# A norm factor that is left out of an MLP's operands and put into the norm behind it, on one Trainium2 core

## The chip, the cores and the metric

The kernel runs on one core of a Trainium2 chip. The core has a matrix engine (PE, TensorE), a vector engine (DVE), an activation engine (ACT, ScalarE), a general engine (POOL, GpSimd), and SyncE (SP), which issues most of the transfers (DMA) between device memory and the on-chip memory (SBUF). Each engine takes its instructions in the order of the program; semaphores hold an instruction back until its operands are there and the place it writes is free. The metric is the time of one execution on the device in microseconds (us).

## What is computed

Two layers of a streaming encoder for 1024 + 32 tokens of width 1024: a forgetting attention (FoX), then a gated linear recurrence (HGRN2), each followed by an MLP with a squared ReLU and hidden width 4096. Cut to what the change touches, for each layer:

```python
def rmsnorm(x, g):
    return x * lax.rsqrt(jnp.mean(x * x, axis=-1, keepdims=True) + EPS) * g

x = x + rmsnorm(out, post_mix_norm[layer])     # out: the mixer's output projection
h = rmsnorm(x, pre_ffn_norm[layer])            # x * r * gain, r one number per token
u = jax.nn.relu(h @ ffn_w_up[layer])
x = x + rmsnorm((u * u) @ ffn_w_down[layer], post_ffn_norm[layer])
```

With r left out of h, relu(x * gain @ W) is smaller by r and its square by r squared, and the norm behind the MLP can make up for that: the mean of squares is multiplied by the fourth power of r ahead of the root, and its factor by r squared.

## The kernel before

Tokens lie along the free axis, features on the partitions. The 1056 tokens are four blocks of G = 264; half c (0 or 1) of the tokens is two of them (h = 0, 1), so that an operation on one feature tile of one half is 128 x 528. Everything that the change touches is in `tail`, which runs once behind each mixer: output projection, norm of the mixer, input norm of the MLP, MLP, norm behind it.

*The MLP.* The products go by a scheme of seven products on 2 x 2 blocks (Strassen's), each product in three passes on split operands (high times high, high times low, low times high). A half's input has four pairs of feature tiles (kp = 0 to 3). `forms` makes, for each pair, the scaled tiles (a DVE operation with the gain of the feature and the factor r of the token), four differences (`t_forms`) and the split into high (a cast on ACT) and low (DVE): the tile F[c][kp], 2 x 7 x 264 wide. `unit` runs the seven products, `unit8` (for half 0's first NA = 5 units, and half 1's last steps) the same matrix in eight plain products, m by m. `block` issues the matmuls, `cut` splits weights into S. The 16 units of the up projection go: units 0 to 4 on half 0 alone (`up8`), then unit i on both halves with unit i - 5 on half 1. Results, squared, go as forms to device memory (`uf`), and `get_forms` fetches them in four parts for each pair and half (forms 0-1, 2-3, 4-5, 6) through four landing places in the tile st. The four slots of F for each half are used again, pair p in slot p % 4. `down` has 19 steps: 0 to 13 on both halves, 14 to 18 on half 0, then `down8` 14 to 18 on half 1.

*The factor.* `sums` (called cs in the profile) adds the squares over the partitions with a matmul against ones; `factor` takes the root: two ACT operations and three on DVE for each block, and with `sc` (a factor of the mixer's own, in layer 1) three DVE operations more. `postnorm` goes over the eight feature tiles: scale (DVE), add to x (DVE), square the new x (ACT), add the square to a sum (DVE).

*The order around the change.* The output projection of half 0 goes first, then column 0 of half 1's, then half 0's factor and `postnorm` on DVE while PE goes on with columns 1 to 4. Then cs for the second factor stands on PE between columns 4 and 5, `forms` of half 0 comes on DVE and ACT, PE goes on with columns 5 to 7 and begins unit 0. Half 1's factor stands in unit 0, its second between units 1 and 2; its forms must be there at unit 5. At the end of the MLP half 0's norm runs while half 1's last steps are on PE; `next_h` makes the next mixer's input. A scheduler lays the instructions out; `soon` gives priority, `behind` and `pin` fix an order by hand.

## Time and profile before

| | |
|---|---|
| median of 3 runs | 3012.45 us (3007.43 to 3015.72) |
| the profiled execution | 3009.45 us, its span 3007.7 us |
| busy: PE, DVE | 2845.7 us (95%), 2053.5 us (68%) |
| busy: ACT, POOL | 1472.0 us (49%), 1468.6 us (49%) |
| waits of PE for F casts (L316), for squares ahead of cs, for the first result of half 1 in `down` | 15.5, 34.4, 15.2 us |
| transfers | 349.36 MB, 116 GB/s on the mean |

The profile page gives each engine's busy time and the span in 40 slices; the trace behind it answers for any stretch. Three views carry what follows. A table by windows has the busy time and the number of instructions of each engine in a stretch, the granted clock of PE as a share of its full 2.4 GHz, and the transfers. A timeline has one engine's instructions in order, each with the idle time before it and what ended that. A view of one source line has the durations of its operations by shape.

### The profile page before, as it was taken

What the parts mean: (1) busy time and instruction counts of PE and PEld (TensorE: products, weight loads), DVE (VectorE), ACT (ScalarE), POOL (GpSimd) and SP (SyncE); (2) the same over time, 40 slices, a digit from 0 to 9 for tenths busy, and PEclk for the clock granted to TensorE, in tenths of its full rate; (3) what the DMA queues carried; (4) which work ended last, traced back from release to release, by engine and by line L of the source; (5) the groups of instructions that cost most, each with busy time, mean ns of one, the idle gap of its engine ahead of it and who ended that gap; (6) DMA issues with size and microseconds to landing.
All of it is one profiled execution on the core that took longest, in us unless ns stands there. A gap on an engine that the chain in (4) does not pass through costs nothing.

```text
span 3007.7 us, 56032 instructions
## 1 busy us (share of the span) xinstructions
PE 2845.7 (95%) x21377; PEld 2725.1 (91%) x21377; DVE 2053.5 (68%) x3419; ACT 1472.0 (49%) x3104; POOL 1468.6 (49%) x1595
## 2 busy tenths in 40 slices
PE   7999999999889998999979999999988999899987
PEld 6888888899889998999869999999988999799986
DVE  6788888864785545678888655546488554667787
ACT  6455555555455655544454232322345665644443
POOL 2344444431227775466723644544314886556660
PEclk9999999999989999999989999999999999899997
DMA  5111211144434445445353211115444443544452
GB/s 163 47 48 46 55 46 48 52 113 142 137 129 173 158 145 183 153 132 152 111 161 118 57 56 40 48 33 150 145 126 161 154 166 144 192 143 135 148 166 76
DMA packets 329172, 349.36 MB, mean 116 GB/s; under 512 B 19535, under 2 KB 287703, under 8 KB 328903
## 3 DMA queue, kind: packets, MB, share of 16 engines
q1 hardware_dynamic: 327879, 345.65, 36.6%
q8 instruction: 168, 2.75, 0.4%
q14 instruction: 101, 0.83, 0.1%
q0 software_dynamic: 1024, 0.13, 0.0%
HBM read 238.78 MB, written 106.88 MB: 115 GB/s over the span
## 4 chain that ended last, share of the span: by engine, by line
PE 70%; DVE 13%; DMA 5%; ACT 4%; issue 4%; POOL 4%; SPq 0%; DVEq 0%; ACTq 0%; POOLq 0%
PE mA L410 14%; PE mB L410 11%; PE hj L184 8%; PE pj L184 8%; PE mE L410 5%; PE gp L184 4%; PE po L184 4%; DMA st<-uf 2%; DVE S L398 2%; PE mD L410 1%; DVE F L317 1%; PE lv L1465 1%; POOL hs L310 1%; PE pv L1129 1%; PE ss L1002 1%
## 5 line engine op out<-in xcount | busy, mean ns | idle before, releaser
L410 PE MATMUL mA<-F,S 128*128 128x264 f32 x4404 | 604.8, 289 | 50.3 <-ACT F L316 15.5
L410 PEld LDWEIGHTS mA<-F,S 128*128 128x128 f32 x4404 | 566.0, 191 | 62.8 <-ACT F L316 17.2
L410 PE MATMUL mB<-F,S 128*128 128x264 f32 x4248 | 585.5, 287 | 11.1 <-DVE S L398 4.8
L410 PEld LDWEIGHTS mB<-F,S 128*128 128x128 f32 x4248 | 548.4, 191 | 17.5 <-DVE S L398 9.0
L398 DVE TENSOR_TENSOR S<-Sx,S 128x512 fp32r<-128x512 f32 (+3 forms) x280 | 247.6, 889 | 157.3 <-ACT S L397 155.0
L398 DVE TENSOR_TENSOR S<-raw,S 128x512 fp32r<-128x512 f32 (+3 forms) x282 | 240.4, 857 | 89.6 <-ACT S L397 89.5
L317 DVE TENSOR_TENSOR F<-st,F 128x528 fp32r<-128x528 f32 (+2 forms) x260 | 229.1, 885 | 100.0 <-ACT F L316 99.3
L316 ACT CAST F<-st 128x528 fp32r<-128x528 f32 (+2 forms) x260 | 153.6, 596 | 252.4 <-DMA st<-uf 238.6
L410 PE MATMUL mE<-F,S 128*128 128x264 f32 x1740 | 246.4, 289 | 17.9 <-DVE S L398 9.3
L184 PE MATMUL pj<-H,wh 128*128 128x352 f32 x1152 | 256.7, 341 | 2.1 <-POOL wh L163 1.5
L336 POOL TENSOR_TENSOR Sx<-raw 128x512 f32<-128x512 f32 (+3 forms) x140 | 187.9, 1345 | 132.1 <-DVE S L398 129.6
L410 PEld LDWEIGHTS mE<-F,S 128*128 128x128 f32 x1740 | 225.3, 190 | 26.2 <-DVE S L398 14.5
L310 POOL TENSOR_TENSOR hs<-hs 128x264 f32<-128x264 f32 x216 | 188.4, 891 | 103.5 <-ACT hs L549 101.0
L184 PE MATMUL hj<-h,wh 128*128 128x264 f32 x1600 | 228.7, 289 | 0.0
L170 POOL TENSOR_SCALAR wh<-wr 128x1024 fp32r<-128x1024 f32 x58 | 69.0, 1190 | 319.2 <-PE hj L184 100.2
L184 PEld LDWEIGHTS pj<-H,wh 128*128 128x128 f32 x1152 | 199.8, 192 | 19.0 <-POOL wh L163 1.7
L200 POOL TENSOR_TENSOR e<-e,Y 128x264 f32<-128x264 f32 x170 | 164.0, 974 | 102.1 <-ACT e L741 87.3
L171 DVE TENSOR_TENSOR wl<-wr,wh 128x1024 fp32r<-128x1024 f32 x102 | 135.3, 1328 | 111.1 <-POOL wh L170 59.4
L184 PEld LDWEIGHTS hj<-h,wh 128*128 128x128 f32 x1600 | 206.1, 189 | 1.6
L397 ACT CAST S<-Sx 128x512 fp32r<-128x512 f32 (+3 forms) x280 | 163.6, 585 | 51.3 <-PE mE L410 22.1
L397 ACT CAST S<-raw 128x512 fp32r<-128x512 f32 (+3 forms) x282 | 161.3, 574 | 45.4 <-PE mB L410 32.5
L1125 DVE TENSOR_TENSOR pl<-pf,ph 128x512 fp32r<-128x512 f32 x192 | 127.6, 669 | 54.2 <-POOL ph L1124 29.7
(351 smaller groups left out, 5879.0 us busy)
## 6 DMA issues: line engine op xcount, KB each, us to landing
st<-uf SPq DMA_DIRECT2D x192, 264.0 KB
uf<-hs SPq DMA_DIRECT2D x54, 924.0 KB
raw<-in_ffn_w_up_dram SPq DMA_DIRECT2D x40, 1024.0 KB
raw<-in_ffn_w_down_dram SPq DMA_DIRECT2D x30, 1024.0 KB
wr<-in_hgrn_w_in_dram SPq DMA_DIRECT2D x39, 512.0 KB
wr<-in_fox_w_in_dram SPq DMA_DIRECT2D x32, 512.0 KB
uf<-us SPq DMA_DIRECT2D x10, 924.0 KB
st<-uf SPq DMA_DIRECT2D x64, 132.0 KB
```

The lines of the kernel that those rows point to most:

```text
L170: self.g.tensor_scalar(out=wh, in0=raw, scalar1=1.0, scalar2=0.0, op0=ALU.mult, op1=ALU.add)
L171: self.v.tensor_tensor(wl, raw, wh.bitcast(F32), op=ALU.subtract)
L184: ins = self.nc.tensor.matmul(ps, lhsT=ws[kk][a], rhs=xs[kk][b], start=i == 0, stop=i == tot - 1)
L200: self.g.tensor_tensor(out, a, b, op=op)
L310: ins = e.tensor_tensor(f[:, o], f[:, a], f[:, b], op=ALU.subtract)
L316: self.s.copy(hi, src)
L317: self.v.tensor_tensor(lo, src, hi.bitcast(F32), op=ALU.subtract)
L336: self.g.tensor_tensor(src, a, b, op=op)
L397: self.s.copy(hi, src)
L398: self.v.tensor_tensor(lo, src, hi.bitcast(F32), op=ALU.subtract)
L410: ins = self.nc.tensor.matmul(o, lhsT=a[:, i], rhs=F[kp % 4][:, b, f], start=start and n == 0, stop=stop and n == tot - 1, skip_group_chec ...
L1125: self.v.tensor_tensor(pl[:, :N], pf[:, :N], ph[:, :N].bitcast(F32), op=ALU.subtract)
```

## The change

1. `forms` no longer takes r. It runs for one pair; the scaling by the gain alone is an ACT copy with a scale. For half 0, pairs 0 and 1 are made inside `postnorm` (through the new argument `then`), pairs 2 and 3 directly behind it. All of half 1's projection columns run without a cs in between.
2. `square_factor` makes r, squares it with one DVE operation and keeps it in the tile rq. For half 0 its cs comes behind the projection, for half 1 behind unit 4. `factor` behind the MLP takes it as `sc`.
3. At the first step of `down` the parts are fetched in another order: the parts of forms 0 and 1 of pairs 0 and 1 and of both halves first.
4. Half 1's pairs 14 and 15 are fetched in three parts each (forms 0, 1, 2 and 4, all that `down8` reads), and pair 15's go to places of pairs 13 and 14 that are no longer read (`moved`, `operand`), ahead of the half-0 steps.
5. `next_h(0)` goes into the middle of `down8(16)` (through `mid`).
6. The weights of the last step go to the upper rows of the buffer that the step before uses. The tile rr has one buffer where it had three.

```diff
@@ -281,6 +282,9 @@
                     todo[j - 1] = self.square(c, x[:, j - 1, sl], j - 1, hs, tmp)
             if j >= 2 and more:
                 put(todo[j - 2](self.v))
+            if then and 1 < j <= NJ and j % 2 == 0:
+                for ins in then(j // 2 - 1):
+                    put(ins)
 
     def xd_view(self):
         return self.xd.rearrange("p j (h c t) -> p j h c t", h=2, c=2)
...
-                                                  op0=ALU.mult, op1=ALU.mult)
-                if last:
-                    self.behind(ins, last)
-            last = self.t_forms(f, (self.v, self.v, self.v, self.v))
-            self.F[c].append(place(kp))
-            self.split(self.F[c][kp], f[:, 0:7], 0, 7)
+
+    def forms(self, c, x, kind, layer, kp, f, F):
+        for j, o in ((2 * kp, f[:, 0:8:7]), (2 * kp + 1, f[:, 2:5:2])):
+            self.s.activation(o, x[:, j], AF.Copy, scale=self.gcol(kind, layer, j))
+        ins = self.t_forms(f, (self.v, self.v, self.v, self.v))
+        self.F[c].append(F)
+        return ins, self.split(F, f[:, 0:7], slice(0, 7))
 
 
 
...
@@ -387,6 +386,9 @@
                 if e == 1:
                     with self.soon():
                         evac(m, e, 1, z)
+                    if m == 0 and self.mid:
+                        f, self.mid = self.mid, None
+                        f(self.last_mm)
 
     def bank(self, tag):
...
 
 
+    def operand(self, F, kp, b, f):
+        if F is self.F[1] and (kp, f) in self.moved:
+            kp, f = self.moved[kp, f]
+        return F[kp % 4][:, b, f]
+
...
         for a, b in ((hi, 1), (lo, 1), (hi, 0)):
             for i, kp in enumerate(pairs):
-                ins = self.nc.tensor.matmul(o, lhsT=a[:, i], rhs=F[kp % 4][:, b, f], start=start and n == 0,
...
 
+            r2 = [tp.tile([128, 2, G], F32, name=f"rq{layer}_{c}") for c in range(2)]
+
+            def square_factor(c, late):
+                r = self.factor(self.acc(c), late=late, r=r2[c])
+                self.v.tensor_tensor(r, r, r, op=ALU.mult)
+
...
             with ExitStack() as c2:
                 ob = self.pool(f"ob{layer}", 1, ctx=c2, side="right")
-                ya = new(fa, "ya", 28)
-                ys = [pair(ya)]
-                xa = pair(new(fa, "xa", 16))
-
-                scr = [ob.tile([128, 8, G], F32, name=f"fs{layer}_{i}") for i in range(2)]
+                ys = [pair(new(fa, "ya", 16))]
+                scr = new(fa, "fs", 8)
+                new(fa, "pad", 4)
+                xa = new(ob, "xa", 16)
+                xw, xa = xa[:, 0:8], pair(xa)
 
                 def project(c, os, hs=(0, 1)):
                     for o in os:
...
                 self.get_x(0, xa)
-                scs = sc and sc(0)
+                scs = sc and sc(0, r2[0])
                 project(0, range(NJ))
                 ys.append(pair(new(self.rh if last else ob, "yb", 16)))
                 late = project(1, range(1))
                 fr = self.factor(self.acc(0), scs, late=late)
                 self.pin(self.last_cs)
-                self.postnorm(0, ys[0], xa, fr, 1, layer)
+
+                put = lambda kp: self.forms(0, xa, 2, layer, kp, scr if kp < 3 else xw, form_tile(fa))
+                self.postnorm(0, ys[0], xa, fr, 1, layer, then=lambda kp: put(kp) if kp < 2 else ())
                 self.put_x(0, xa)
-                late = project(1, range(1, 5))
-                r = self.factor(self.acc(0), late=late)
-                self.pin(self.last_cs)
-                self.forms(0, xa, r, 2, layer, lambda kp: scr[kp % 2], lambda kp: form_tile(fa))
-                project(1, range(5, NJ))
+                put(2)
+                put(3)
+                square_factor(0, project(1, range(1, NJ)))
 
 
                 xb = pair(new(self.rh, "xb", 16))
...
                 up8(0, ust, lambda m: first[m])
-                fr = self.factor(self.acc(1), sc and sc(1), late=self.mid_mm)
+                fr = self.factor(self.acc(1), sc and sc(1, r2[1]), late=self.mid_mm)
                 self.pin(self.last_cs)
...
-                if i == 1:
-                    r = self.factor(self.acc(1), late=self.last_mm)
-                if i == 2:
-                    self.pin(self.last_cs)
             with self.soon():
-                self.forms(1, xb, r, 2, layer, lambda kp: (fscr, st)[kp % 2], lambda kp: form_tile(fb, tag=f"f{kp}"))
+                for kp in range(4):
+                    self.forms(1, xb, 2, layer, kp, fscr, form_tile(fb, tag=f"f{kp}"))
+            square_factor(1, self.last_mm)
             n = [0]
 
```

```diff
 
-            def get_forms(p, c, n=4):
-                for a, b in ((0, 2), (2, 4), (4, 6), (6, 7)):
+            PARTS = ((0, 2), (2, 4), (4, 6), (6, 7))
+
+            def get_forms(p, c, parts=PARTS):
+                for a, b in parts:
                     self.nl += 1
-                    i = 8 - 2 * (self.nl % n + 1)
+                    i = 8 - 2 * (self.nl % 4 + 1)
                     t = st[:, i:i + b - a]
                     nc.sync.dma_start(t, self.uf[p][c][:, a:b])
-                    self.split(self.F[c][p % 4], t, a, b)
+                    F, o = self.F[c][p % 4], slice(a, b)
+                    if c and (p, a) in self.moved:
+                        q, o = self.moved[p, a]
+                        F, o = self.F[c][q % 4], slice(o, o + 1) if b == a + 1 else slice(o, o + 3, 2)
+                    self.split(F, t, o)
 
...
             for s in range(LAG):
-                for p in range(4) if s == 0 else (s,) if s > 3 else ():
+                if s == 0:
+
+                    for p, part in zip((0, 1, 0, 1, 2, 0, 0, 1, 1, 2, 2, 2, 3, 3, 3, 3),
+                                       (0, 0, 1, 1, 0, 2, 3, 2, 3, 1, 2, 3, 0, 1, 2, 3)):
+                        for c in range(2):
+                            get_forms(p, c, parts=(PARTS[part],))
+                elif s > 3:
                     for c in range(2):
-                        get_forms(p, c)
+                        get_forms(s, c)
                 down(s, (0, 1), load)
-            get_forms(LAG, 1)
+            few = ((0, 2), (2, 3), (4, 5))
+            get_forms(LAG, 1, parts=few)
+
+            self.moved = {(15, 0): (14, 3), (15, 1): (14, 5), (15, 2): (14, 6), (15, 4): (13, 6)}
+            get_forms(15, 1, parts=few)
             for s in range(LAG, 19):
                 if s < 16:
                     get_forms(s, 0)
-                down(s, (0,), load)
-
-
+                down(s, (0,), load if s < 18 else lambda src: load(src, 4))
+
+
+            new(fa, "pad", 28)
             xs = [pair(new(fa, "xs", 16)) for c in range(2)]
             for c in range(2):
...
+            fr = self.factor(self.acc(0), r2[0], late=self.mid_mm)
             self.postnorm(0, Y[0], xs[0], fr, 3, layer, more=not last)
             down8(15, 1, load2)
             if last:
                 self.store_y(0, xs[0], yring)
             else:
-                next_h(0, self.last_mm)
+                self.mid = lambda late: next_h(0, late)
             for s in range(16, 19):
-                down8(s, 1, load2)
+                down8(s, 1, load2 if s < 18 else lambda src: load2(src, 4))
             if last:
                 fr = None
                 for h in range(2):
-                    fr = self.factor(self.acc(1), r=fr, hs=(h,))
+                    fr = self.factor(self.acc(1), r2[1], r=fr, hs=(h,))
                     self.postnorm(1, Y[1], xs[1], fr, 3, layer, more=False, hs=(h,))
                     self.store_y(1, xs[1], yring, (h,))
                 return
@@ -815,7 +846,7 @@
             self.cut(w0[1], w0[0], raw)
             c4.close()
             late = self.hgrn_early(w0, ev)
-            fr = self.factor(self.acc(1), late=late[0])
+            fr = self.factor(self.acc(1), r2[1], late=late[0])
```

On PE in layer 0 the middle of half 1's projection stood like this before (po: a column's result, H and wh, wl: operands of the projection, cs: the sum of squares):

```order
L184 MATMUL po_9692<-H_78,wl_9663 128x264 x8
L184 MATMUL po_9692<-H_79,wh_9662 128x264 x8
L219 MATMUL cs_9721<-st_8881,ones 128x264
L219 MATMUL cs_9729<-st_8881,ones 128x264
L184 MATMUL po_9779<-H_78,wh_9775 128x264 x8
L184 MATMUL po_9779<-H_78,wl_9776 128x264 x8
```

and the start of the MLP behind the projection (F_918 to F_921: half 0's pairs 0 to 3, mA, mB, mE: products of unit 0):

```order
L184 MATMUL po_9925<-H_78,wl_9896 128x264 x8
L184 MATMUL po_9925<-H_79,wh_9895 128x264 x8
L410 MATMUL mA_9966<-F_918_9743,S_9964 128x264
L410 MATMUL mA_9966<-F_919_9752,S_9964 128x264
L410 MATMUL mB_9967<-F_918_9743,S_9964 128x264
L410 MATMUL mB_9967<-F_919_9752,S_9964 128x264
L410 MATMUL mE_10026<-F_918_9743,S_9964 128x264
L410 MATMUL mE_10026<-F_919_9752,S_9964 128x264
L410 MATMUL mB_10027<-F_918_9743,S_9964 128x264
L410 MATMUL mB_10027<-F_919_9752,S_9964 128x264
L410 MATMUL mA_9966<-F_920_9761,S_9964 128x264
L410 MATMUL mB_9967<-F_920_9761,S_9964 128x264
```

With the change the projection's end and the start of the MLP stand like this (F_903 to F_906: pairs 0 to 3):

```order
L185 MATMUL po_9910<-H_78,wl_9881 128x264 x8
L185 MATMUL po_9910<-H_79,wh_9880 128x264 x8
L220 MATMUL cs_9938<-st_8881,ones 128x264
L220 MATMUL cs_9946<-st_8881,ones 128x264
L418 MATMUL mA_9968<-F_903_9456,S_9966 128x264
L418 MATMUL mA_9968<-F_904_9473,S_9966 128x264
L418 MATMUL mA_9968<-F_905_9500,S_9966 128x264
L418 MATMUL mB_9969<-F_903_9456,S_9966 128x264
L418 MATMUL mB_9969<-F_904_9473,S_9966 128x264
L418 MATMUL mB_9969<-F_905_9500,S_9966 128x264
L418 MATMUL mE_10028<-F_903_9456,S_9966 128x264
L418 MATMUL mE_10028<-F_904_9473,S_9966 128x264
```

The cs has moved behind the whole projection, and the first nine matmuls use pairs 0 to 2 where the first eight used pairs 0 and 1.

On DVE, the part of half 0's forms before (rr: the second factor, L298: the scaling, L310: a difference, L317: a low part, wl: a weight's low part for the projection):

```order
L211 SCALAR_TENSOR_TENSOR rr_9720<-rt_9723,rr_9720 128x264
L209 SCALAR_TENSOR_TENSOR rt_9731<-cs_9729,rr_9720 128x264
L252 TENSOR_TENSOR st_8881<-st_8881 128x528
L210 SCALAR_TENSOR_TENSOR rt_9731<-rt_9731,rr_9720 128x264
L211 SCALAR_TENSOR_TENSOR rr_9720<-rt_9731,rr_9720 128x264
L298 SCALAR_TENSOR_TENSOR fs_0_8887<-xa_867_8886,gain,rr_9720 128x2x264 x2
L310 TENSOR_TENSOR fs_0_8887<-fs_0_8887 128x264 x2
L171 TENSOR_TENSOR wl_9896<-wr_9893,wh_9895 128x1024
L310 TENSOR_TENSOR fs_0_8887<-fs_0_8887 128x264 x2
L298 SCALAR_TENSOR_TENSOR fs_1_8888<-xa_867_8886,gain,rr_9720 128x2x264 x2
L310 TENSOR_TENSOR fs_1_8888<-fs_1_8888 128x264 x3
L317 TENSOR_TENSOR F_918_9743<-fs_0_8887,F_918_9743 128x1848
```

and with the change (L277 and L280: the scaling and the addition of `postnorm`, L309: differences, L316: low parts, L253: a sum of squares):

```order
L277 SCALAR_TENSOR_TENSOR ya_866_8887<-ya_866_8887,gain,rr_9432 128x528
L280 TENSOR_TENSOR xa_869_8890<-xa_869_8890,ya_866_8887 128x528
L172 TENSOR_TENSOR wl_9641<-wr_9638,wh_9640 128x1024
L309 TENSOR_TENSOR fs_867_8888<-fs_867_8888 128x264 x4
L172 TENSOR_TENSOR wl_9701<-wr_9698,wh_9700 128x1024
L316 TENSOR_TENSOR F_903_9456<-fs_867_8888,F_903_9456 128x1848
L277 SCALAR_TENSOR_TENSOR ya_866_8887<-ya_866_8887,gain,rr_9432 128x528
L280 TENSOR_TENSOR xa_869_8890<-xa_869_8890,ya_866_8887 128x528
L253 TENSOR_TENSOR st_8881<-st_8881 128x528
L277 SCALAR_TENSOR_TENSOR ya_866_8887<-ya_866_8887,gain,rr_9432 128x528
L280 TENSOR_TENSOR xa_869_8890<-xa_869_8890,ya_866_8887 128x528
L172 TENSOR_TENSOR wl_9761<-wr_9758,wh_9760 128x1024
```

Pairs 0 and 1 stand inside `postnorm`, ahead of any factor of the second norm, and no scaling is left on DVE.

On ACT at the end of the up projection before (F_918, F_919: half 0's slots of pairs 0 and 1, F_976: half 1's of pair 0; L316: high part of a fetched part; L548, L549, L587: results of the up projection):

```order
L316 CAST F_918_9743<-st_8881 128x528
L587 COPY e_13769<-mB_13756 128x264
L587 COPY e_13784<-mB_13771 128x264
L397 CAST S_9964<-Sx_9965 128x512 x2
L316 CAST F_918_9743<-st_8881 128x528
L316 CAST F_976_10675<-st_8881 128x528
L587 COPY e_13831<-mA_13722 128x264
L587 COPY e_13845<-mA_13737 128x264
L397 CAST S_9964<-raw_934_9962 128x512
L316 CAST F_976_10675<-st_8881 128x528
L548 ACTIVATE hs_982_10707<-hs_982_10707 128x2x264
L397 CAST S_9964<-raw_935_9963 128x128
```

and with the change (F_903, F_904 and F_972, F_973: pairs 0 and 1 of half 0 and half 1; L315: high part):

```order
L315 CAST F_903_9456<-st_8881 128x528
L315 CAST F_904_9473<-st_8881 128x528
L597 COPY e_13771<-mB_13758 128x264
L315 CAST F_972_10654<-st_8881 128x528
L315 CAST F_973_10663<-st_8881 128x528
L597 COPY e_13786<-mB_13773 128x264
L399 CAST S_9966<-Sx_9967 128x512 x2
L315 CAST F_903_9456<-st_8881 128x528
L597 COPY e_13833<-mA_13724 128x264
L597 COPY e_13847<-mA_13739 128x264
L399 CAST S_9966<-raw_935_9964 128x512
L315 CAST F_904_9473<-st_8881 128x528
```

The first four casts are of four different slots, where the first two were of one.

## Rows read from the trace of the kernel before

**Rows 1.** Windows: us, PE, PEld, DVE, ACT, POOL busy (instructions), PEclk, DMA share, GB/s

```profile
780.00:920.00 140.00, 116.43 (x898) 113.63 (x897) 116.71 (x165) 71.06 (x131) 45.55 (x33) 0.93 0.46 152
774.00:818.00 44.00, 42.16 (x342) 41.48 (x342) 40.48 (x55) 20.68 (x40) 13.59 (x9) 1.00 0.40 123
940.00:960.00 20.00, 20.00 (x167) 20.00 (x166) 8.78 (x14) 11.62 (x24) 14.00 (x15) 1.00 0.37 139
2200.00:2340.00 140.00, 119.65 (x886) 115.38 (x885) 116.64 (x172) 76.12 (x141) 48.50 (x38) 0.91 0.42 138
1180.00:1240.00 60.00, 45.68 (x322) 43.09 (x321) 43.73 (x74) 35.35 (x89) 26.45 (x29) 0.86 0.63 202
2580.00:2640.00 60.00, 46.01 (x329) 42.90 (x328) 44.74 (x75) 36.53 (x89) 27.48 (x31) 0.86 0.72 230
1540.00:1580.00 40.00, 25.09 (x160) 22.48 (x160) 37.59 (x68) 19.93 (x40) 5.80 (x5) 0.83 0.33 101
```

**Rows 2.** Timeline of PE, layer 0, behind the projection: start, us, work [idle before]

```profile
828.35 0.59 PE L410 MATMUL mA<-F,S 128*128 128x264 f32 x1 [5.77 <-ACT F L316]
...
832.93 2.13 PE L410 MATMUL mA<-F,S 128*128 128x264 f32 x8 [3.34 <-ACT F L316]
...
868.25 2.12 PE L219 MATMUL cs<-st,ones 128*128 128x264 f32 x4 [5.58 <-DVE st L252]
...
910.28 1.24 PE L410 MATMUL mA<-F,S 128*128 128x264 f32 x8 [2.10 <-ACT F L316]
```

**Rows 3.** Timeline of PE, the same place in layer 1

```profile
2240.57 1.91 PE L410 MATMUL mA<-F,S 128*128 128x264 f32 x7 [2.63 <-ACT F L316]
...
2279.65 2.13 PE L219 MATMUL cs<-st,ones 128*128 128x264 f32 x4 [8.01 <-DVE st L252]
```

**Rows 4.** Views of single lines: count, min/median/max ns, first and last start, shape

```profile
L298 DVE SCALAR_TENSOR_TENSOR fs<-xa,gain,rr x16: 754/760/1851, 807.6 to 2234.2; 128x528 f32<-128x528 f32 x16
L298 DVE SCALAR_TENSOR_TENSOR fs<-xb,gain,rr x8: 753/766/1259, 873.9 to 2299.7; 128x528 f32<-128x528 f32 x8
...
L310 DVE TENSOR_TENSOR fs<-fs x48: 416/422/1501, 810.7 to 2305.5; 128x264 f32<-128x264 f32 x48
...
L316 ACT CAST F<-fs x12: 1722/1732/1747, 813.5 to 2306.7; 128x1848 fp32r<-128x1848 f32 x12
...
L317 DVE TENSOR_TENSOR F<-fs,F x12: 2065/2070/2083, 815.8 to 2312.7; 128x1848 fp32r<-128x1848 f32 x12
...
L251 ACT ACTIVATE st<-xa x14: 634/646/650, 782.8 to 2208.0; 128x528 f32<-128x528 f32 x14
...
L211 DVE SCALAR_TENSOR_TENSOR rr<-rt,rr x32: 421/432/1448, 777.5 to 2987.2; 128x264 f32<-128x264 f32 x32
```

**Rows 5.** Timeline of DVE in layer 0, end of half 0's and of half 1's norm

```profile
797.28 0.69 DVE L279 TENSOR_TENSOR xa<-xa,ya 128x528 f32<-128x528 f32 x1
...
865.58 0.70 DVE L279 TENSOR_TENSOR xb<-xb,yb 128x528 f32<-128x528 f32 x1
```

**Rows 6.** Timeline of ACT in layer 0, start of the down projection

```profile
1168.07 0.64 ACT L316 CAST F<-st 128x528 fp32r<-128x528 f32 x1
...
1173.73 0.64 ACT L316 CAST F<-st 128x528 fp32r<-128x528 f32 x1
...
1198.49 2.31 ACT L316 CAST F<-st 128x528 fp32r<-128x528 f32 x4 [3.52 <-DMA st<-uf]
1202.68 0.38 ACT L712 COPY Y<-mA 128x264 f32<-128x264 f32 x1 [1.88 <-DMA uf<-hs]
...
1227.38 0.41 ACT L316 CAST F<-st 128x264 fp32r<-128x264 f32 x1 [3.11 <-DMA st<-uf]
```

**Rows 7.** Timeline of PE in layer 0, the same place

```profile
1203.11 1.03 PE L410 MATMUL mA<-F,S 128*128 128x264 f32 x3 [7.48 <-ACT Y L712]
```

**Rows 8.** DMA view of 1170 to 1230 us: what was moved, in 40 slices

```profile
GB/s 282 266 391 406 264 61 198 249 274 241 83 226 173 223 207 90 404 228 363 399 434 280 330 85 204 145 320 342 281 43 177 183 90 70 271 346 263 199 11 96
```

**Rows 9.** Timeline of PE in layer 0, end of the MLP

```profile
1553.36 2.13 PE L219 MATMUL cs<-st,ones 128*128 128x264 f32 x4 [6.78 <-DVE st L252]
```

More of the change, by code (lines that the diff above doesn't have):

```diff
@@ L76, in __init__ @@
         self.pp = self.pool("pp", 1, PSUM)
-        self.table = self.pinned = None
+        self.table = self.pinned = self.mid = None
+        self.moved = {}
         nc.scalar.preload_act_table_set(TABLE)
@@ L259, in get_x, with postnorm @@
             self.nc.sync.dma_start(x[:, j:j + 4], self.xd_view()[:, j:j + 4, :, c])
-    def postnorm(self, c, y, x, fr, kind, layer, more=True, hs=(0, 1), tmp=None):
+    def postnorm(self, c, y, x, fr, kind, layer, more=True, hs=(0, 1), tmp=None, then=None):
         sl = slice(hs[0], hs[-1] + 1)
```

31 lines of the change are left out of this document (13 added, 18 removed).

## The prediction, on record before the changed kernel ran

> **What bounds the kernel.** I read the page's busy times and slices first: TensorE (PE) is busy nearly all the time, so the kernel is a row of matmuls, and what can be won is the time in which they don't flow. The table by windows shows where that is. A full window has 167 matmuls in 20 us, 0.1198 us each. In each of the stretches below I take the length less 0.1198 us for each matmul counted as what is lost [rows 1]. Behind the first output projection (780 to 920) it is 140 - 898 x 0.1198 = 32.4 us, in the second layer (2200 to 2340) 140 - 886 x 0.1198 = 33.9. Twelve column-sum matmuls in each of these, 2.12 us for four [rows 2], stay as they are: 12 x (0.53 - 0.12) = 4.9. That leaves 27.5 and 29.0 to win (**stretch A**). At the start of the down projection (**stretch B**) it is 60 - 322 x 0.1198 = 21.4 and 60 - 329 x 0.1198 = 20.6. At the end of layer 0 (**stretch C**, 1540 to 1580) it is 40 - 160 x 0.1198 = 20.8.
>
> Next the PE timeline of these stretches, for what ended each wait. In A of layer 0, PE waits 5.77 and 3.34 us for ScalarE's (ACT's) casts of half 0's forms, then 5.58 us before a column sum (cs) that needs half 1's squares, then 2.10 us for half 1's forms [rows 2]. The granted clock of the stretch is 0.93 on the mean [rows 1], so part of it ran at the lower of PE's two levels, 1.2 instead of 2.4 GHz. Layer 1 has the same waits, 2.63 and 8.01 us the largest [rows 3]. VectorE (DVE) and ACT aren't full over A: 116.7 and 71.1 of 140 us [rows 1].
>
> **Forms without the factor: stretch A.** Before, half 0's forms start only when the factor r is there, and r needs a stop of PE in the middle of half 1's projection. From the first scaling (L298, 807.6 [rows 4]) to pair 3's arrival at 832.93 [rows 2] four pairs take 25 us. The change makes pairs 0 and 1 inside the post-mix norm, pair 2 directly behind, so that pair 3 alone is late. DVE ended that norm at 798 before [rows 5]. Three pairs cost DVE four subtractions (0.42) and a low part (2.07) each [rows 4]: 3 x 3.8 = 11.3, so 809. Pair 3's subtractions and its high part are 4 x 0.42 + 1.73 = 3.4 more, so 813 at the earliest. To this come two or three weight casts (wl) on DVE, DVE's operations that take longer than their median, and what is ahead in ACT's queue (squares of half 1 at 0.64 each): 816 to 821. I take the late end, 821, since these queues are served in program order. The projection itself ends about 2.5 us sooner, because the column sum that stood in it comes behind it. So PE begins the MLP at 818 with three pairs, nine matmuls deep, and stands up to 3 us for pair 3: **832.9 - 821 = 12 us**, and with the long stand the half clock goes too, which I count at nothing.
>
> The second stop, 5.58 us before the column sum between units 1 and 2, goes: that sum, now only for r squared, stands behind unit 4. Half 1's forms must be there when PE comes to unit 5. Half 1's new x was complete at about 866 [rows 5] and will be at 854. A pair costs two scalings on ACT (0.65), four subtractions, the high and the low part: 1.3 + 1.7 + 1.7 + 2.1 = 6.8 us, one pair after the other, since all four now use one scratch tile: 27 us, until 881. Before, the four took from 873.9 [rows 4] to 910.28, 36 us, with two scratch tiles; by that it is 890. PE asked for the last pair 2.10 us ahead of 910.28, at 908.2, and asks now 12 + 5.6 sooner, at 890.6. It is close: 0 to 3 us of wait. **Layer 0: 12 + 5.6 = 17.6, I take 18; the bounds are 9 (the second stop comes back as a wait at unit 5) and 24 (the small waits go as well).** Layer 1 by the same steps: pair 3 about 9 us sooner than 2240.57, and 8.01 us of the second stop: 17, with part of the column sum's wait in the projection **18**, bounds 9 and 25.
>
> Load on the engines: 16 scalings per layer leave DVE, 0.76 us each by the median and up to 1.85 [rows 4], and come to ACT. ACT's price for a scaled copy of this size isn't in the trace; its squares of 128x528 at 0.64 us are the nearest row and what I take, the 0.76 of the operation it replaces is the upper bound. DVE gains 12.2 us and gives back 2 x 0.9 for r squared (as two operations of 0.43 on half the size): some 106 of 122 us. ACT has 71 + 16 x 0.65 = 81 of 122. Neither is full, but DVE isn't far off.
>
> **The order of loads: stretch B.** In the ACT timeline the first casts of the fetched forms come at 1168.07 and 1173.73: the four landing places all hold parts of pair 0, half 0, whose later parts can be cast only when unit 15 has left forms 2 to 6 of that slot. Then ACT stands 3.52 us for data, four casts later the first copy of half 1's result goes out, and PE, which stood for that bank, starts again 7.48 us late [rows 6, 7]. With the parts of forms 0 and 1 of two pairs and both halves first, four casts can go at about 1168, and four more by 1174 to 1176, where there were two or three. That is five parts ahead. There are 32 parts between 1168 and 1228 [rows 6], or 1.9 us a part: nine us ahead at best. The copy still stands behind some 21 casts, as it did behind 20, so no more than that is won. I take **8 us a layer, 16 in all**, bounds 0 and 12 each.
>
> Is it the transfers themselves? The two stretches moved 202 and 230 GB/s [rows 1], and in 1170 to 1230 the DMA view has slices of 1.5 us between 11 and 434 [rows 8]: it comes in bursts, as a ring of four places would have it, not at a ceiling. The Trainium skill (SBUF — State Buffer, section "A bandwidth-pool intuition that's wrong (but worth ruling out)") puts the path between memory and one core at about 358 GB/s. By that page too, 230 is no ceiling and the order can matter; the trace's best slices lie above its figure, and the measurement decides. Were 230 a ceiling, B would give nothing (the second rival).
>
> **The end of the MLP: stretch C.** Three things. (1) The factor behind the MLP takes r squared: three more DVE operations of 0.43 for each block (the size of L211's [rows 4]), one of which can run early. Two blocks: 1.7 us on the chain of each factor that PE waits for. At the very end of the program the second block's lie beside the first block's norm: +0.9 us. (2) Half 1's pair 15 is fetched in three parts into places that others left, ahead of the half-0 steps. Four low parts leave the crowded stretch around 1530 and run now beside the half-0 steps, where DVE has room; no large wait of PE hangs on them, so I count nothing. (3) Half 0's sum for the next layer is put 36 matmuls (4.4 us) later: of the 6.78 us wait at 1553.36 [rows 9] about 4 are filled. But DVE is busy 37.6 of 40 us here [rows 1], and its chain (norm, next input, half 1's squares) decides when half 1's sum can come. What PE does earlier it waits for later. So: gain 0 to 5 in layer 0 from (3), loss 1.7 + 0.9 + 1 (the same again behind the first of the two factors) from (1): **0, bounds -4 and +4.** The tile rr now has one buffer, and the last weights go to the upper rows of a used one; the next user comes whole steps later, so I count nothing.
>
> **Sum.** 18 + 18 + 16 + 0 = 52 us. 3009.45 - 52 = 2957.5 for the profiled execution, which lay 3.0 below the median: **2960**.
>
> **Rivals.**
> *One scratch binds (A).* If the chain of half 1's forms is much longer than 6.8 us a pair, because DVE's subtractions stand behind weight cuts and squares, then PE waits at unit 5 for what the second stop cost: A gives 9 a layer, the sum is 34, 2978. For it: 27 to 36 us in a space of 36 is thin, and single subtractions took 1.5 us [rows 4]. Against it: ACT and DVE have 13% to 30% free.
> *Transfers bind (B).* B gives nothing: 36, 2976. Both rivals together: 18, 2994.
> *Slower: the projection starves.* DVE was busy 40 of 44 us in half 1's projection already [rows 1], and now makes three pairs (11.3 us) in it, before weight casts that PE's next column needs. The seven remaining columns of each layer each wait for one. If each comes late by more than 52 / 14 = 3.7 us, all is lost; at 5 us it is 18 us slower, 3030. Against it: the stretch held four scalings, six subtractions, a low part and a factor before, 4 x 0.76 + 6 x 0.42 + 2.07 + 6 x 0.43 = 10.2 us, so it grows by about 1 us.
> *No effect.* The waits move behind the next resource in every stretch: about 3010. Against it: the waits in A hang on r by its data, and r is gone from them.
>
> **Chances.** Forecast, 2948 to 2972: 0.52. One scratch: 0.16. Transfers: 0.13. Both: 0.07. More than forecast, down to 2936 by the upper bounds of A and B: 0.05. Slower: 0.04. No effect: 0.03. What can be told from no change here is about 0.3%, 9 us: faster 0.93, same 0.03, slower 0.04. The range runs from 2938 to 2990: it takes in the first four cases but the worst of "both", and most of the fifth.
>
> **What would show it.** Right: no wait over 4 us for F behind the projection, matmuls flowing by 821 and 2232; no stop before a column sum between units 1 and 2; under 3 us at unit 5; about 0.95 of full flow in 780 to 920. In B the wait for half 1's copy under 2 us, and eight casts by 1176. Wrong: waits of PE for wl in the projection, a wait of 5 us or more for F at unit 5, the same 7 us at the copy, or a chain at the end that is over 3 us longer.

## The result and the profile after

The changed kernel took **2993.16 us** (2991.87 to 2995.34), the one before 3012.54 us (3007.43 to 3015.72) in the same comparison: a ratio of 0.9938, interval 0.9921 to 0.9955. It is faster by 19 us. The forecast was 2960 and the range ended at 2990: the sign was right, the size was not. The profiled execution has a span of 2991.7 us against 3007.7.

Both kernels have 21377 matmuls on PE, in nearly the same order. So the start of the n-th matmul in one trace less its start in the other is a running account of what has been won, and its steps are the terms of the sum. Times in the left column are those of before.

| stretch | won so far, us | in this stretch | forecast |
|---|---|---|---|
| 774, in the first output projection | 0.8 | | |
| A of layer 0 (to 920) | 17.0 | +16.2 | 18 |
| B of layer 0 (1160 to 1240) | 17.4 | +0.4 | 8 |
| C (1540 to 2080) | 17.8 | about 0 | 0 |
| layer 1's mixer (2105 to 2120) | 9.8 | **-7.8** | none |
| A of layer 1 (2120 to 2340) | 16.6 | +6.8 | 18 |
| B of layer 1 (2590 to 2640) | 17.5 | +0.7 | 8 |
| the end (3000) | 16.4 | -1 | 0 |

The windows of the stretches, columns as in [rows 1]; those of B lie 15 us earlier than in [rows 1], as the kernel is ahead there:

```profile
780.00:920.00 140.00, 132.41 (x1027) 129.41 (x1027) 115.48 (x165) 91.06 (x171) 56.24 (x46) 0.96 0.50 164
2200.00:2340.00 140.00, 125.78 (x936) 121.81 (x935) 111.91 (x160) 86.19 (x167) 64.57 (x53) 0.93 0.44 149
1165.00:1225.00 60.00, 45.52 (x324) 43.13 (x323) 39.39 (x70) 34.01 (x84) 27.25 (x30) 0.86 0.57 183
2565.00:2625.00 60.00, 46.76 (x335) 44.11 (x335) 43.00 (x77) 35.55 (x87) 26.68 (x29) 0.86 0.68 223
```

In layer 0's A, 1027 matmuls pass where 898 did. In B hardly anything has changed: 324 for 322, 335 for 329, the clock 0.86 as before.

PE's timeline in layer 0's A, as [rows 2]:

```profile
815.66 0.63 PE L418 MATMUL mA<-F,S 128*128 128x264 f32 x3
...
819.61 1.61 PE L418 MATMUL mA<-F,S 128*128 128x264 f32 x8 [2.28 <-ACT F L315]
...
879.29 1.06 PE L220 MATMUL cs<-st,ones 128*128 128x264 f32 x4
...
887.20 0.63 PE L418 MATMUL mB<-F,S 128*128 128x264 f32 x3 [1.81 <-DVE rt L210]
...
890.34 2.13 PE L418 MATMUL mE<-F,S 128*128 128x264 f32 x8 [1.65 <-DVE S L400]
...
898.41 1.24 PE L418 MATMUL mA<-F,S 128*128 128x264 f32 x8 [1.30 <-ACT S L399]
```

The MLP begins at 815.7 with three pairs, flows from 819.6 (forecast 821), and the column sum between units 1 and 2 is gone: half 1's now stands behind unit 4, at 879, without a wait. By 893 on before's clock the lead was 23.8. Then units 4 and 5 gave back 6.8 us in three waits and at a granted clock of 0.88 (876 to 904).

The same place in layer 1, as [rows 3]:

```profile
2218.21 0.39 PE L418 MATMUL mA<-F,S 128*128 128x264 f32 x1 [1.13 <-ACT F L315]
...
2220.67 1.03 PE L418 MATMUL mB<-F,S 128*128 128x264 f32 x3 [1.82 <-DVE rt L210]
...
2223.78 2.13 PE L418 MATMUL mA<-F,S 128*128 128x264 f32 x8 [2.08 <-ACT F L315]
...
2266.27 3.01 PE L418 MATMUL mA<-F,S 128*128 128x264 f32 x12 [4.60 <-ACT us L577]
```

Here the lead went from 9.8 (2120) to 17.0 behind the projection, 23.8 when the old second stop (8.01 us, [rows 3]) was passed, and back to 16.6 by 2340, most of it in the new wait of 4.60 us for ACT.

And the loss of 7.8 us in layer 1's mixer, on SP's queue and on PE. The kernel after:

```profile
2085.47 2.29 SPq L260 DMA_DIRECT2D xa<-xd  x2
...
2091.64 1.88 SPq L1571 DMA_DIRECT2D go<-odh  x4
...
2101.93 2.87 SPq L1571 DMA_DIRECT2D go<-odh  x4
```

```profile
2100.72 2.13 PE L185 MATMUL gp<-h,wh 128*128 128x264 f32 x8 [7.03 <-DVE gz L1580]
```

and the kernel before:

```profile
2134.33 0.99 SPq L259 DMA_DIRECT2D xa<-xd  x2
```

```profile
2111.85 1.25 PE L184 MATMUL gp<-h,wh 128*128 128x264 f32 x8 [0.55 <-DVE gz L1548]
```

The residual xa (two loads of 1056 KB) is fetched ahead of the parts that the mixer's gate needs (go, 132 KB each), where before it was issued behind all of them. Its tile has moved from the ring fa, whose previous user had to be done first, to the pool ob, which is free early. From 2085 to 2100 us the kernel after moved 343 GB/s, with the DMA engines' busy share at 1.0.

### The profile page after: what moved, and what is told of

Its sections match the earlier page's. It is cut to its first block, busy times and chain, and to the rows that moved or that the text cites. A ratio compares the mean times of both kernels' runs of the same rounds, so it can differ in the third digit from the quotient of the medians.

```text
span 2991.7 us, 56039 instructions
## 1 busy us (share of the span) xinstructions
PE 2845.5 (95%) x21377; PEld 2728.0 (91%) x21377; DVE 2019.0 (67%) x3411; ACT 1500.5 (50%) x3141; POOL 1465.1 (49%) x1586
## 5 line engine op out<-in xcount | busy, mean ns | idle before, releaser
L418 PE MATMUL mA<-F,S 128*128 128x264 f32 x4404 | 607.8, 290 | 47.3 <-ACT Y L733 12.8
L418 PEld LDWEIGHTS mB<-F,S 128*128 128x128 f32 x4248 | 548.5, 191 | 23.6 <-DVE S L400 11.9
L400 DVE TENSOR_TENSOR S<-Sx,S 128x512 fp32r<-128x512 f32 (+3 forms) x280 | 238.8, 857 | 184.2 <-ACT S L399 179.9
L400 DVE TENSOR_TENSOR S<-raw,S 128x512 fp32r<-128x512 f32 (+3 forms) x282 | 232.5, 831 | 101.9 <-ACT S L399 101.4
L316 DVE TENSOR_TENSOR F<-st,F 128x528 fp32r<-128x528 f32 (+1 forms) x252 | 214.4, 858 | 79.0 <-ACT F L315 78.5
L309 POOL TENSOR_TENSOR hs<-hs 128x264 f32<-128x264 f32 x216 | 188.7, 892 | 103.9 <-ACT hs L559 102.2
L315 ACT CAST F<-st 128x528 fp32r<-128x528 f32 (+1 forms) x252 | 142.8, 574 | 191.0 <-DMA st<-uf 180.3
L171 POOL TENSOR_SCALAR wh<-wr 128x1024 fp32r<-128x1024 f32 x49 | 58.5, 1193 | 293.0 <-PE pj L185 99.4
```

Of the source, the lines that this page charges most:

```text
L171: self.g.tensor_scalar(out=wh, in0=raw, scalar1=1.0, scalar2=0.0, op0=ALU.mult, op1=ALU.add)
L309: ins = e.tensor_tensor(f[:, o], f[:, a], f[:, b], op=ALU.subtract)
L315: self.s.copy(hi, src)
L316: return self.v.tensor_tensor(lo, src, hi.bitcast(F32), op=ALU.subtract)
L400: self.v.tensor_tensor(lo, src, hi.bitcast(F32), op=ALU.subtract)
L418: ins = self.nc.tensor.matmul(o, lhsT=a[:, i], rhs=self.operand(F, kp, b, f), start=start and n == 0, stop=stop and n == tot - 1, skip_gro ...
```

## The experiments

Each ratio is to the kernel before, run on the same chip in the same comparison (e1 to e4, e5 to e8 and e9 to e11 are one comparison each, with the kernel before at 3006 to 3008 us). So runs of different comparisons are set side by their ratios, the changed kernel's being 0.9938. e1 to e7 are the changed kernel with one edit more or undone, e8 is the kernel before with one edit; e9 to e11 combine edits.

**e1: xa's load behind the first column of the projection.**

```diff
-                self.get_x(0, xa)
                 scs = sc and sc(0, r2[0])
-                project(0, range(NJ))
+                first = project(0, range(1))
+                self.get_x(0, xa, first)
+                project(0, range(1, NJ))
```

> The changed kernel with one thing altered: the load of half 0's old x (xa, 2 x 1056 KB) is ordered behind the first column of the output projection, where the kernel before issues it, and not among the gates of layer 1's mixer. Theory: the early load delays the gate loads go<-odh behind it on the queue and the transfer engines, and costs the 7.03 us wait before L1580's result at 2100 us. Then that wait falls under 1 us and the time goes from 2993 to about 2986. Rival: the wait is of the engines (POOL or DVE stand behind other work there); then it stays and the time stays within 2 us of 2993. A third: the lead is only taken later by the next wait (the factor's sum in the projection); then the wait goes and the time stays.

Measured: 2980.51 us, ratio 0.9913 (0.9898 to 0.9928). PE's wait for gz has fallen from 7.03 to 1.1 us, and at the matmul where the changed kernel had lost 7.8 us this one has kept them: 22.0 us ahead of before at 2120 against 9.8 (5 of the difference is an earlier lead). By the ratios it gives 7.5 us; their intervals overlap, so it is the trace that tells. The loss came from the load's early place in the queue; whether the parts of go behind it stood in the queue or shared the DMA engines with it, no run took apart.

**e2: the old order of the fetched parts.**

```diff
-                if s == 0:
-
-                    for p, part in zip((0, 1, 0, 1, 2, 0, 0, 1, 1, 2, 2, 2, 3, 3, 3, 3),
-                                       (0, 0, 1, 1, 0, 2, 3, 2, 3, 1, 2, 3, 0, 1, 2, 3)):
...
+                for p in range(4) if s == 0 else (s,) if s > 3 else ():
```

> The changed kernel with the old order of the fetched parts at the first step of the down projection (all parts of pair 0, half 0, then half 1, then pair 1). Prediction: the new order is worth 8 us a layer, so 2993 + 16 = 3009. Theory after the result: it is worth 1 to 2 us a layer, because the wait of PE ends with the copy of half 1's first result (6.83 and 5.95 us after the change, 7.48 and 7.76 before), which stands behind as many casts as before: 2995 to 2997.

Measured: 2990.85 us, 0.9949 (0.9935 to 0.9964), not told apart from the changed kernel. PE's waits for the copies are 15.2 us in two, as before the change; the new order has 12.8. The order is worth 2.4 us in these waits and not more.

**e3: the casts of pairs 2 and 3 behind the matmuls of steps 0 and 1.** With this nothing stands ahead of the first copy of half 1's result in ACT's queue but pairs 0 and 1.

```diff
+                    for p, part in zip((0, 1, 0, 1, 0, 0, 1, 1), (0, 0, 1, 1, 2, 3, 2, 3)):
...
+                elif s < 3:
+                    for c in range(2):
+                        get_forms(s + 1, c, after=self.last_blk)
```

> The changed kernel with the casts of pairs 2 and 3 at the start of the down projection ordered behind the matmuls of its first and second step; those steps read pairs 0 and 1 alone. The copy of half 1's first result then stands behind 16 casts on ACT and not behind 21. Theory (order on ACT): the waits of 6.83 and 5.95 us before that copy fall to 1 to 3 us, and 6 to 10 us are won over both layers: 2983 to 2987. Rival (transfers or the ring of four places set the pace): PE waits as long in sum, at the copy or one step later for pair 2's forms: 2991 to 2996. A worse outcome: pair 3 comes too late and PE waits at the fourth step: over 2998.

Measured: 2982.56 us, 0.9923 (0.9908 to 0.9938). On ACT and on PE:

```profile
1180.76 0.38 ACT L735 COPY Y<-mA 128x264 f32<-128x264 f32 x1 [8.41 <-DMA uf<-hs]
```

```profile
1181.19 1.03 PE L420 MATMUL mA<-F,S 128*128 128x264 f32 x3 [6.56 <-ACT Y L735]
```

ACT stood idle 8.41 us with no cast ahead of the copy, and PE waited as long as ever (6.83 us in the kernel after). So the queue of casts is not what holds the copy: it is a store, uf<-hs. My account of stretch B fell here.

**e4: half of the bytes of the fetched pairs 0 to 3.** It leaves out 132 of their 264 columns.

```diff
+                    wid = G // 2 if p < 4 else G
+                    nc.sync.dma_start(t[:, :, 0:wid], self.uf[p][c][:, a:b, 0:wid])
```

> The changed kernel, but of the parts of pairs 0 to 3 at the start of the down projection only half the columns are fetched (132 of 264 in each form; the casts read old data in the rest), so the result isn't the reference's. All instructions stay. Bytes set the pace: the waits of 6.83 and 5.95 us fall by half or more, 2981 to 2987. The ring of four places and the time from issue to landing set it, or the order on ACT alone: the waits stay within 1.5 us, 2990 to 2994.

Measured: 2987.87 us, 0.9937 (0.9921 to 0.9954). The two waits are 10.1 us, the longest 5.4. The window of B in layer 0, to be read beside the one above:

```profile
1165.00:1225.00 60.00, 47.22 (x343) 44.94 (x343) 40.59 (x74) 36.18 (x90) 27.98 (x30) 0.86 0.49 147
```

All transfers of the window fall by a fifth, from 183 to 147 GB/s, and the DMA engines' share from 0.57 to 0.49; the two waits fall by a fifth too, and the time by nothing that can be told. This speaks against the transfers but doesn't settle it, as the stores have kept their bytes.

**The new account of B.** The ring rh is filled in turn: four staging tiles hs of 8 units, then half 0's result Y (16 units) over the first two of them and half 1's over the last two. Unit 15's forms are staged in the last two. In the kernel after, on POOL, SP and ACT:

```profile
1176.05 2.56 POOL L309 TENSOR_TENSOR hs<-hs 128x264 f32<-128x264 f32 x3
```

```profile
1178.64 0.32 SPq L563 DMA_DIRECT2D uf<-hs  x1
```

```profile
1180.29 2.32 ACT L315 CAST F<-st 128x528 fp32r<-128x528 f32 x4 [4.80 <-DMA st<-uf]
1184.39 0.38 ACT L733 COPY Y<-mA 128x264 f32<-128x264 f32 x1 [1.78 <-DMA uf<-hs]
```

The last difference ends at 1178.6, the store of 924 KB goes out at 1178.64 and lets ACT go at 1184.39, 5.75 us later. In the trace half 1's first copy waits for both of unit 15's stores, this one and the one issued at 1174.97. By the kernel's text the copy writes where the earlier of the two reads, but Y is one tile over both places, and it waits for the later one as well. A later product of PE uses the copy's bank, and so starts at 1184.82, after 6.83 us of waiting.

**e5: Y in two tiles for each half, and the staging tiles taken in another order**, so that what the last stores read lies under features 4 to 7 of Y, which the first step doesn't write.

```diff
-                return hst[n[0] % 4]
+                return hst[(0, 2, 1, 3)[n[0] % 4]]
...
-            Y = [pair(new(self.rh, "Y", 16)) for c in range(2)]
+            class Halves:
+                def __init__(s):
+                    s.t = [new(self.rh, "Y", 8)[:, 0:8].rearrange("p (j h) t -> p j h t", h=2) for i in range(2)]
...
+            Y = [Halves() for c in range(2)]
```

> The changed kernel; the sums Y of the down projection lie on the four tiles hs from which the last up units' results are stored. Each half's Y is cut in two tiles, and the order in which the units take the tiles hs is changed, so that the first step's Y lies where unit 14's results were and not unit 15's, whose store is issued last (1178.64). Theory (a store decides): the copy of half 1's first result waits for no cast but for the store of unit 15's forms out of the place it writes; then the waits of 6.83 and 5.95 us fall under 2 us, and 8 to 12 us are won: ratio to the kernel before 0.990 to 0.991, where the changed kernel has 0.9938. Rival (casts and fetched parts set the pace, the copy's releaser is a misreading): the waits stay in sum, ratio 0.993 to 0.995.

Measured: **2966.68 us, 0.9864 (0.9845 to 0.9882)**. No wait for a copy of Y is left among PE's waits. Windows of B, to be read beside the two above:

```profile
1165.00:1225.00 60.00, 57.00 (x423) 55.34 (x422) 49.83 (x84) 40.90 (x99) 33.47 (x32) 0.91 0.65 208
2565.00:2625.00 60.00, 54.44 (x424) 53.15 (x423) 48.67 (x81) 38.44 (x95) 31.55 (x32) 0.97 0.65 210
```

In 60 us 99 and 89 matmuls more: 11.9 and 10.7 us at 0.1198 each. The same casts, copies and transfers are in it. It shows the stores under Y as the cause, and the 208 GB/s in the window of layer 0, where the kernel after had 183, that the transfers were at no ceiling. The edit cuts Y in two and changes the order of the staging tiles; what either does alone wasn't run.

**e8: the same two edits on the kernel before.**

> The kernel before with the places of Y alone changed as in e5 (two tiles for each half, on the places of unit 14's results for the first step). Theory (a store decides): its waits of 7.48 and 7.76 us before the copy of half 1's first result fall under 3 us, and 8 to 13 us are won without any other edit: ratio 0.996 to 0.997. Rival: with the old order of the fetched parts the parts bind instead, and less than 3 us are won: over 0.999.

Measured: 2986.33 us, 0.993 (0.9913 to 0.9947): 21 us, about as much as the whole change gave. The lead over before goes from 2.6 to 13.6 in B of layer 0, and from 12.7 to 23.6 in layer 1.

**e6: without half 1's squares in the mixer's norm.** It leaves out that sum, so r squared of half 1 is not the right one; all that uses it is still done.

```diff
-                self.postnorm(1, ys[1], xb, fr, 1, layer)
+                self.postnorm(1, ys[1], xb, fr, 1, layer, more=False)
```

> The changed kernel without the squares of half 1's new x in the norm of the mixer (eight squares on ACT and seven additions on DVE or POOL in each layer are left out; the factor of the MLP's norm then comes from old sums, so the result isn't the reference's). Theory (the stop before the column sum has only moved into ACT's queue, where the copies out of PSUM stand behind squares that wait for DVE): the 4.60 us wait before a copy at 2266 in layer 1 goes, PE's waits before unit 5 in both layers fall, and 8 to 14 us are won: ratio 0.989 to 0.991. Rival (DVE's other work, the norm and the forms, is what is late): 0 to 4 us, ratio 0.9925 to 0.994.

Measured: 2977.78 us, 0.9903 (0.9888 to 0.9918), 10.5 us less than the changed kernel by the ratios. What is left of the waits at unit 5 in layer 0 and for ACT in layer 1:

```profile
889.31 1.24 PE L418 MATMUL mA<-F,S 128*128 128x264 f32 x8 [0.45 <-ACT S L399]
...
2251.96 1.72 PE L418 MATMUL mA<-F,S 128*128 128x264 f32 x12 [1.02 <-ACT us L577]
```

Of layer 0's 6.8 us given back nothing is left, of the 4.60 us 1.02. These squares and their sums are what costs behind the second stop. The gain is as expected, but the way isn't quite the one expected. On ACT in the kernel after:

```profile
2264.65 0.64 ACT L252 ACTIVATE st<-xb 128x528 f32<-128x528 f32 x1 [1.87 <-DVE xb L280]
2265.83 0.39 ACT L577 ACTIVATE us<-mA 128x264 f32<-128x264 f32 x1 [0.54 <-DVE xb L280]
```

and in e6:

```profile
2251.52 0.39 ACT L577 ACTIVATE us<-mA 128x264 f32<-128x264 f32 x1 [2.63 <-DVE xb L280]
```

The result of the up projection that PE waits for (us<-mA) is itself let go by the norm's last addition to xb on DVE. So it is in e6, where no square stands ahead of it and ACT is idle for 2.63 us. The squares delay it through DVE, where their sums stand between the norm's additions: the last addition ends at 2265.80 in the kernel after and at 2251.49 in e6, 14.3 us sooner, where the matmuls shortly before it were 10.9 sooner. Why this result depends on that addition isn't shown.

**e7: the end of the MLP as before** (half 0's next input at its old place, pair 15 fetched whole and late).

> The changed kernel with its end as before: half 0's next input directly behind the step 15, and half 1's pair 15 fetched in four parts behind step 14 into two landing places. The prediction counted these two edits at nothing, -4 to +4 us; the lead over the kernel before is 17 to 18 us on both sides of that stretch. Expected: within 3 us of the changed kernel, ratio 0.993 to 0.995. Rival: the deferral of the next input holds 4 us that another cost hides; then the ratio rises over 0.995.

Measured: 2989.06 us, 0.9939 (0.9922 to 0.9956), as the changed kernel. Its column sum there waits longer and earlier:

```profile
1532.58 2.13 PE L220 MATMUL cs<-st,ones 128*128 128x264 f32 x4 [9.84 <-DVE st L253]
```

and in the kernel after 4.00 us follow two waits for DVE:

```profile
1531.39 1.25 PE L418 MATMUL mA<-F,S 128*128 128x264 f32 x4 [3.20 <-DVE S L400]
1536.65 2.13 PE L220 MATMUL cs<-st,ones 128*128 128x264 f32 x4 [4.00 <-DVE st L253]
```

By the starts of the same matmuls the changed kernel gains 6.0 us on e7 by 1538, and has lost 4.4 of them by 1561 and all by 1600. What the filled wait wins is waited for again on DVE.

**e9: e1 and e5 together.**

> The changed kernel with two edits together: the load of xa ordered behind the first column of the projection, and half 1's result Y in two tiles with the four hs tiles in the order 0, 2, 1, 3. If the two waits are independent stretches (theory), the ratios add: 0.9913 + 0.9864 - 0.9938 = 0.984, some 2959 us against 3007, a lead over the changed kernel of 12 at the second layer's projection, of which 9 to 11 us of stage B come twice. Rival: work won ahead is waited for again at the next DVE- or ACT-bound stretch (the first layer's end, the second layer's norm), as was seen in stretch C and in the second layer's stretch A; then only the larger of the two is left, 0.986 to 0.987.

Measured: 2961.56 us, 0.985 (0.9834 to 0.9867), where the sum of the two gives 0.9839. They add, within the interval. It beats both kernels.

**e10: e9 with e3's casts.**

> The same, and the casts of the fetched pairs 2 and 3 behind the matmuls of steps 0 and 1 of the down projection. With the copies at Y out of the way, theory A: the 3.7 us that this order gave before were won apart from those copies, in the steps behind them: 0.983. Rival: with Y no longer waiting, steps 0 and 1 reach pairs 2 and 3 sooner, and these now come late: PE waits for F casts in steps 2 and 3, 2 to 6 us a layer, 0.985 to 0.988.

Measured: 2962.71 us, 0.9855 (0.9841 to 0.987): nothing on top of e9. The 4 us that this order showed in e3 are either part of what e5 wins or within the scatter of the runs; this isn't settled.

**e11: e9 with half 1's squares behind its forms.**

```diff
+                self.postnorm(1, ys[1], xb, fr, 1, layer, more=False)
...
+            for j in range(NJ):
+                self.square(1, xb[:, j], j)(self.v)
             square_factor(1, self.last_mm)
```

> The kernel e9 (late xa, Y in two tiles), and half 1's squares of the mixer's norm taken out of the norm's loop and put behind half 1's forms (the same sum is computed, later). Leaving them out altogether was worth 10.5 us. Theory: they cost because ACT's queue stands behind them while DVE's additions come, so moved they cost little: 0.981 (8 us less than e9). Rival: the eight squares and seven sums, some 5 us each on ACT and DVE, now hold up unit 5's forms or its results' stores, and the gain is 0 to 3 us, or a loss, as the wait at the sum behind unit 4 moves.

Measured: 2958.18 us, 0.9845 (0.9831 to 0.986): 3.4 us less than e9 by the medians and 1.5 by the ratios, not told apart from it. In PE's timeline the wait for ACT in layer 1 is down to 1.02 us, and one of 2.85 us for DVE stands at unit 4 in layer 0:

```profile
887.35 1.24 PE L420 MATMUL mE<-F,S 128*128 128x264 f32 x8 [2.85 <-DVE S L402]
...
2241.11 3.01 PE L420 MATMUL mA<-F,S 128*128 128x264 f32 x12 [1.02 <-ACT us L579]
```

In layer 1 the wait fell from 4.58 us in e9, but the stretch from 2270 to 2345 (times of before) takes 73.3 us for e9's 72.6: what the place gave was waited for elsewhere. In layer 0 the stretch from 893 to 925 takes 35.9 us for 38.5. Left out of the changed kernel, the squares gave 10.5 us; put later in e9, 1.5 to 3.4. So it is mainly their work on DVE and ACT in this stretch that costs, and less their place. The rival of this run was right.

## Why the prediction was off, step by step

*Stretch A, layer 0: right.* Pair 3 at 819.6 for 821, a stand of 2.28 us for "up to 3", the second stop gone: +16.2 for 18. What went on inside was larger both ways. Restart and stop gave some 23, as the upper bound had it, and units 4 and 5 took 6.8 back where 0 to 3 us were allowed. The allowance looked at the forms alone (27 to 36 us for four pairs). But PE's three waits there are not for F: they are for the factor's operation on DVE (rt) and for cuts of weights (S). With the squares and their sums left out 0.45 us of these waits remain (e6); r squared is still made there, and its share isn't known.

*The term of half 1's forms: mis-sized.* It was 6.8 us a pair. In layer 1 the first scaling starts at 2266.39 and the last low part ends at 2305.8:

```profile
2266.39 1.36 ACT L300 ACTIVATE fs<-xb,gain 128x528 f32<-128x528 f32 x2
```

```profile
2303.73 2.08 DVE L316 TENSOR_TENSOR F<-fs,F 128x1848 fp32r<-128x1848 f32 x1
```

That is 39.4 us, 9.9 a pair, and each pair's scaling starts within 1.2 us of the low part of the pair ahead: the one scratch tile binds, as the first rival had it. Its wait didn't come with it. In e6 the chain is as long (39.3 us) and PE waits 0.80 us for F behind it, in the kernel after 0.30.

*Stretch A, layer 1: the term that was mis-sized, +6.8 for 18.* The projection without its column sum gave 17.0 - 9.8 = 7.2; the restart kept its waits (1.13, 1.82, 2.08), one of them for the factor's operation on DVE, since the sum now stands there, and took 1.8 back: 5.4 for 9. The second stop gave 23.8 - 15.2 = 8.6 for 8. Then 7.2 were lost by 2340. The step that failed is "the stop goes": half 1's norm on DVE, which PE had waited for at the column sum, was not shortened, and a result on ACT that PE needs waits for the same norm's last addition (e6). PE was 15.1 us ahead there and that addition only 11.8 (2265.80 for 2277.61). I counted the busy time of ACT and DVE (81 and 106 of 122 us) and not when the norm ends and who else waits for it.

*Stretch B: wrong in its cause, +1.1 for 16.* "The copy still stands behind some 21 casts" took the casts that lie ahead of the copy for what it waits for. The row itself named another: `1.88 <-DMA uf<-hs` [rows 6], a store, not a load. e3 took the casts away and the wait stayed, e4 halved the loads and a fifth of it went, e5 took the stores away from under what the first step writes and it went. The second rival had the right result (B gives nothing) and a wrong reason: the transfers aren't at a ceiling, since e5 moves more in the same time without the wait. The Trainium skill's figure that was weighed there (SBUF — State Buffer, "A bandwidth-pool intuition that's wrong (but worth ruling out)") thus decides nothing here; e5, with 208 and 210 GB/s in the same windows and no wait for the copy, agrees with it that no ceiling was near.

*Layer 1's mixer: not in the sum, -7.8.* The text went through the tiles that lose a buffer (rr, the last weights) and counted nothing for them; it didn't go through the tiles that change their pool. xa's load, which a busy ring had held back, was free to go early, ahead of loads that PE needed on the same queue. e1 shows it.

*Stretch C: right, 0.* e7 undoes its second and third edit and nothing changes in the time; the first, r squared in the factor, wasn't undone by a run. *The projection starves: no.* PE has no wait for wl in it.

The sum: -1.8 (A), -7.6 (B), -7.8 (mixer), -11.2 (A), -7.3 (B) make up 35.7 of the 36 us by which the profiled execution's gain of 16.0 fell short of 52. That the time came out where the worst rival, both together, had put it (2994) is luck: B gave nothing for another reason, and the mixer's 7.8 us were in no rival. e9 then reaches 2961.56 against 3006.18 in its own comparison, 44.6 us: most of the forecast's gain was there to be had, but with two more edits of places and not for the reasons given.

Four smaller figures of the prediction were off without moving the forecast. 36 matmuls are 4.3 us and not 4.4. Four column sums take 1.06 us where PE hasn't just waited (at 879 above) and not 2.12. ACT's scaled copy of 128x528 took 0.73 us, between the 0.65 taken and the bound of 0.76. The gain by the upper bounds leads to 2936 from the profiled execution; from the median, on which the forecast stands, it is 2939.

## What to carry to other kernels

When a copy out of PSUM is late, read what releases it before counting what is ahead of it in its queue: here a tile that lay over two still being stored waited for both stores, and other places for it were worth as much as the rewrite (21 us). When a tile moves to another pool, ask what used to hold its load back, and what the load now overtakes on its queue (8 us here). When a stop is taken away, look for whoever else waits for the work it waited for; of 8.6 us won at the second stop in layer 1, 7.2 were paid again within 80 us.

## What the runs showed of the hardware

Here a wait cost more than its length. After the wait of 4.60 us in the kernel after and the 1.02 us at the same matmul in e6, ten us of each by windows (columns as in [rows 1]), the kernel after first:

```profile
2266.00:2276.00 10.00, 9.73 (x63) 9.73 (x64) 7.80 (x13) 8.85 (x17) 2.94 (x4) 0.75 0.71 249
```

```profile
2252.00:2262.00 10.00, 9.64 (x77) 9.43 (x78) 7.30 (x12) 8.56 (x16) 4.74 (x4) 1.00 0.90 299
```

The granted clock is 0.75 on the mean behind the long wait, part of it at 1.2 GHz, and 1.00 behind the short one: 14 matmuls fewer, 14 x 0.1198 = 1.7 us on top of the wait.

And some of DVE's operations on operands in SBUF nearly double in length while POOL works. In the kernel after, POOL and DVE in layer 1's norm:

```profile
2255.05 4.53 POOL L309 TENSOR_TENSOR us<-us 128x264 f32<-128x264 f32 x3 [3.72 <-ACT us L582]
2269.51 0.76 POOL L309 TENSOR_TENSOR us<-us 128x264 f32<-128x264 f32 x1 [9.94 <-ACT us L582]
```

```profile
2254.68 0.70 DVE L280 TENSOR_TENSOR xb<-xb,yb 128x528 f32<-128x528 f32 x1
...
2255.90 0.70 DVE L253 TENSOR_TENSOR st<-st 128x528 f32<-128x528 f32 x1
...
2257.70 1.26 DVE L280 TENSOR_TENSOR xb<-xb,yb 128x528 f32<-128x528 f32 x1
...
2261.34 0.70 DVE L280 TENSOR_TENSOR xb<-xb,yb 128x528 f32<-128x528 f32 x1
```

The same addition takes 1.26 us for 0.70 in between, and POOL's three differences take 4.53 us where one by itself takes 0.76. Not every operation is hit: the sum at 2255.90 lies within POOL's 4.53 us too and takes 0.70. The Trainium skill (SBUF — State Buffer, section "🔬 SBUF: two separate sides") says that DVE and POOL share one pair of ports by an exclusive lock, held for a whole instruction; these rows fit it; no run here took the two engines apart.
